# Winograd convolution on one core: the last stores of the seventh pair cut by rows and by channels

## The chip, the cores and the metric

The kernel runs on one core of one Trainium2 chip. The metric is the device time of one execution in microseconds (us), taken as a median over several executions. One further execution was recorded by the hardware profiler; every duration of an instruction, a transfer or a packet comes from it.

## The reference

A batch of 16 images of 64 channels, 64 by 64 pixels, is convolved with 128 filters of 64 channels, 3 by 3, with a border of one zero pixel. All is float32 in memory.

```python
batch, c_in, h, w, c_out = 16, 64, 64, 64, 128
x_pad = np.pad(x, ((0, 0), (0, 0), (1, 1), (1, 1)), mode='constant')
for b in range(batch):
    for co in range(c_out):
        for ci in range(c_in):
            for kh in range(3):
                for kw in range(3):
                    output[b, co] += weight[co, ci, kh, kw] * x_pad[b, ci, kh:kh+h, kw:kw+w]
```

The input has 16.8 MB, the output 33.6 MB.

## The kernel before, in words

Images are worked on in eight pairs (`p` from 0 to 7). The 64 channels of the first image of a pair lie on partitions 0 to 63, those of the second on 64 to 127 (`b2` is the image in the pair). Down the rows, a small Winograd scheme makes two output rows out of sums and differences of input rows: three matmul groups for each block of 16 output rows give `U` (from `ss`, sums of neighbouring rows), `A` and `Bt` (from `xs`, the rows in float16). ScalarE copies `U` into `ut` (L169), VectorE adds it to `A` for the even rows (L178) and to `Bt` for the odd rows (L181). The result lies in `ots[b2]`, one buffer for each image: 128 output channels on 128 partitions, with 64 rows of 64 float32 (16,384 bytes) on each. A pair has four blocks (`blk` 0 to 3, 16 rows each).

Loads: the first two pairs come in float32 by SyncE's queue (SP); the others are loaded by GpSimd's queue (POOL), which turns them into float16 on the way.

Stores: function `store` (L110) sends rows `lo` to `hi` of all 128 channels of one image. The first image of a pair goes out on SP, right after the block that makes its last row. The second image goes out on ScalarE's queue (ACT): it is put in the list `held` and issued in the next block, behind the copies of `U`. `cuts_of` (L108) says for each pair after which block which rows are sent: the first six pairs send each image whole (2 MB) after block 3. The seventh pair (`p = 6`) sends both images in halves (1 MB after block 1, 1 MB after block 3). The last pair (`p = 7`) sends its first image in three pieces (32, 16 and 16 rows after blocks 1, 2 and 3) and its second in halves.

The order of the instructions on each engine follows the order of the program; `keep` fixes it where it is called. The transfers on SP and ACT take turns over eight completion semaphores, so a transfer waits for the one that was issued eight such transfers before it. The eight output buffers are shared with the two float32 inputs, so pair `p` writes into the buffers of pair `p - 4`; the buffers of the last four pairs are not used again.

Of the kernel before, what the change touches and what calls it, by code (L numbers as in the profile page):

```python
# [13 lines left out]
def kernel(  # L14
# [6 lines left out]
    nc = tc.nc  # L21
    B, CI, H, W = x.shape
    CO = weight.shape[0]
    assert H == 64 and W == 64 and CI == 64 and CO == 128 and B % 2 == 0
    NP = B // 2
    RB = 8

    keep = tc.keep_in_program_order
    x_rows = x.rearrange("b c h w -> (b c) h w")
    out_rows = out.rearrange("b co h w -> b co h w")  # L30
# [24 lines left out]
    def load(p):  # L55
        xs[p] = xpool.tile([128, H, W], F16, tag="xs", name="xs")
        keep(nc.gpsimd.dma_start(xs[p], x_rows[128 * p : 128 * p + 128, :, :]))  # L57
# [8 lines left out]
    def sums(eng, p, src, lo, n):  # L66
        if p not in ss:
            ss[p] = spool.tile([128, H // 2, W], F16, tag="ss", name="ss")
        v = src.rearrange("p (j i) c -> p j i c", i=2)
        keep(  # L70
            eng.tensor_add(  # L71
                ss[p][:, lo : lo + n, :], v[:, lo : lo + n, 0, :], v[:, lo : lo + n, 1, :]
            )
        )
# [29 lines left out]

    whole = {3: (0, 64)}
    halves = {1: (0, 32), 3: (32, 64)}
    tail = {1: (0, 32), 2: (32, 48), 3: (48, 64)}
    cuts_of = [(whole, whole)] * (NP - 2) + [(halves, halves), (tail, halves)]  # L108

    def store(eng, p, b2, ot, lo, hi):  # L110
        return eng.dma_start(
            out_rows[2 * p + b2, :, lo:hi, :],
            ot.rearrange("p j i c -> p (j i) c")[:, lo:hi, :],
        )

    for p in range(NP):
        if p > 0 and p + 4 < NP:
            load(p + 4)
        if p + 1 < NP:
            for lo in (0, 16):  # L120
                sums(nc.gpsimd, p + 1, x1 if p == 0 else xs[p + 1], lo, 16)
        ots = [
            opool.tile([128, H // 2, 2, W], F32, tag="ot", name="ot") for _ in range(2)
        ]
        for blk in range(4):
            j0 = blk * RB

            def group(wi_rows):

                tiles = [  # L130
                    psum.tile([128, RB, W], F32, tag="acc", name="acc") for _ in range(2)
                ]
                n = 3 * len(wi_rows)
                i = 0
                for wi, off in wi_rows:
                    for kw in (1, 0, 2):
                        c_lo, c_hi = max(0, 1 - kw), min(W, W + 1 - kw)
                        for b2 in range(2):
                            p0 = 64 * b2
                            lo, hi = j0, j0 + RB  # L140
                            if off is None:
                                rhs = ss[p][p0 : p0 + 64, lo:hi, c_lo + kw - 1 : c_hi + kw - 1]
                            else:
                                while 2 * lo + off < 0:
                                    lo += 1
                                while 2 * (hi - 1) + off > H - 1:
                                    hi -= 1
                                first = 2 * lo + off
                                last = 2 * (hi - 1) + off
                                rhs = xs[p][  # L150
                                    p0 : p0 + 64,
                                    first : last + 1 : 2,
                                    c_lo + kw - 1 : c_hi + kw - 1,
                                ]
                            nc.tensor.matmul(  # L155
                                tiles[b2][:, lo - j0 : hi - j0, c_lo:c_hi],
                                Wt[p0 : p0 + 64, wi, kw, :],
                                rhs,
                                start=i == 0,
                                stop=i == n - 1,  # L160
                            )
                        i += 1
                return tiles

            U = group([(G1, None)])
            us = []
            for b2 in range(2):
                ut = upool.tile([128, RB, W], F32, tag="ut", name="ut")
                keep(nc.scalar.copy(ut, U[b2]))  # L169
                us.append(ut)  # L170
            while held:
                keep(store(nc.scalar, *held.pop(0)))
            if p == 0 and blk >= 2:
                for lo in (32 * blk - 64, 32 * blk - 48):
                    keep(nc.scalar.copy(xs[1][:, lo : lo + 16, :], x1[:, lo : lo + 16, :]))  # L175
            A = group([(G21, 1), (G0, -1)])
            for b2 in range(2):
                nc.vector.tensor_add(ots[b2][:, j0 : j0 + RB, 0, :], A[b2], us[b2])  # L178
            Bt = group([(G01, 0), (G2, 2)])
            for b2 in range(2):  # L180
                nc.vector.tensor_add(ots[b2][:, j0 : j0 + RB, 1, :], Bt[b2], us[b2])  # L181
            if blk in cuts_of[p][0]:
                store(nc.sync, p, 0, ots[0], *cuts_of[p][0][blk])
            if blk in cuts_of[p][1]:
                held.append((p, 1, ots[1], *cuts_of[p][1][blk]))
    while held:
        keep(store(nc.scalar, *held.pop(0)))
# [30 lines left out]
```

## Time and profile before

| what | value |
|---|---|
| median of 3 runs | 127.26 us (127.18 to 127.57) |
| profiled execution: its own time | 128.39 us |
| profiled execution: span, first to last instruction | 126.6 us |
| TensorE matmuls | 106.0 us busy, 84% of the span |
| VectorE | 83.6 us, 66% |
| ScalarE | 44.5 us, 35% |
| GpSimd | 34.6 us, 27% |
| last instruction of VectorE | starts at 115.77, takes 0.68 us |
| last store issued on SP / on ACT | 115.88 / 116.48 us |
| bytes moved, 16 DMA engines | 44.48 MB, mean 351 GB/s |

The profile has five views that matter here. The table in 40 slices shows how busy each engine and the mean of the 16 DMA engines are, 3.2 us to a slice. The list of DMA queues counts packets: q1 is SP's queue, q10 ACT's, q0 GpSimd's; a packet is one run of bytes that one DMA engine moves, and a transfer ends with one packet of 4 bytes on each DMA engine that took part. The chain of waits follows the work that ended last back in time. The table by stretch gives the DMA share (1.00 is all 16 DMA engines busy, so 0.0625 is one of them) for any stretch of time; a packet is counted in the stretch in which it begins, so values a little over 1 occur. The list of transfers gives the median time from issue to landing.

### The profile page before, as it was taken

How to read it: one execution, taken by the hardware profiler on the slowest of the kernel's cores; microseconds unless marked ns; L12 is line 12 of the kernel's file. 1: busy time of each engine (PE TensorE's matmuls, PEld its weight loads, DVE VectorE, ACT ScalarE, POOL GpSimd, SP SyncE). 2: the span in 40 equal slices, each digit the busy share in tenths (PEclk: the TensorE clock that was granted, in tenths of full speed). 3: DMA queues.
4: the chain of work that ended last, by engine and by line, in shares of the span. 5: the costliest groups of instructions: out<-in, count | busy, mean ns of one | idle time of the engine just before them, and what ended most of it. 6: DMA issues, size and time to landing. Idle time of an engine off the chain costs nothing.

```text
span 126.6 us, 2412 instructions
## 1 busy us (share of the span) xinstructions
PE 106.0 (84%) x978; PEld 54.3 (43%) x978; DVE 83.6 (66%) x134; ACT 44.5 (35%) x76; POOL 34.6 (27%) x27
## 2 busy tenths in 40 slices
PE   0407999999999999999999999999999999993000
PEld 0303454554555555554555545455554555541000
DVE  0009297787778777877787778777877787777000
ACT  4108937953333333333333333333333333330000
POOL 2700008677007700699770039000000000000000
PEclk9999999999999999999999999999999999999955
DMA  5999999999999999999999999999999999999970
GB/s 148 370 352 331 342 290 210 215 238 318 383 334 331 295 331 357 365 365 344 349 349 362 383 427 419 419 424 450 419 424 419 432 422 414 430 427 418 418 302 22
DMA packets 4330, 44.48 MB, mean 351 GB/s; under 512 B 480, under 2 KB 480, under 8 KB 864
## 3 DMA queue, kind: packets, MB, share of 16 engines
q1 hardware_dynamic: 2016, 21.27, 40.6%
q10 hardware_dynamic: 1440, 16.78, 31.7%
q0 software_dynamic: 864, 6.29, 24.1%
q8 instruction: 7, 0.11, 0.3%
q14 instruction: 3, 0.02, 0.0%
HBM read 17.07 MB, written 33.55 MB: 400 GB/s over the span
## 4 chain that ended last, share of the span: by engine, by line
PE 82%; DMA 7%; DVE 2%; issue 1%; DVEq 0%; SPq 0%
PE acc L155 82%; DMA x<-in_x_dram 7%; DVE ot L178 1%; DVE ss L71 1%; DVE ot L181 0%; DVEq L213 0%; SPq L42 0%; DVEq L178 0%
## 5 line engine op out<-in xcount | busy, mean ns | idle before, releaser
L155 PE MATMUL acc<-xs,Wt 64*128 64x504 f16 (+3 forms) x768 | 88.9, 378 | 0.0
L155 PEld LDWEIGHTS <-Wt 64*128 64x128 f16 x960 | 53.2, 95 | 55.9 <-issue 6.8
L178 DVE TENSOR_TENSOR ot<-acc,ut 128x512 f32<-128x512 f32 x64 | 41.2, 686 | 23.2 <-PE acc L155 18.5
L169 ACT COPY ut<-acc 128x512 f32<-128x512 f32 x64 | 34.4, 589 | 60.8 <-issue 38.5
L181 DVE TENSOR_TENSOR ot<-acc,ut 128x512 f32<-128x512 f32 x64 | 41.1, 685 | 0.0
L155 PE MATMUL acc<-ss,Wt 64*128 64x504 f16 (+1 forms) x192 | 27.0, 384 | 4.6 <-DVE ss L71 4.6
L71 POOL TENSOR_TENSOR ss<-xs 128x1024 f16<-128x1024 f16 x12 | 25.2, 2122 | 10.1 <-DMA xs<-in_x_dram 9.1
L71 DVE TENSOR_TENSOR ss<-x 128x512 f16<-128x512 f32 x4 | 2.6, 686 | 9.6 <-DMA x<-in_x_dram 9.6
L71 POOL TENSOR_TENSOR ss<-x 128x1024 f16<-128x1024 f32 x2 | 4.7, 2356 | 13.4 <-DMA x<-in_x_dram 13.4
L57 POOL DMA_DIRECT2D xs<-in_x_dram x6 | 3.5, 578 | 17.9 <-PE acc L155 16.0
L96 ACT CAST xs<-x 128x1024 f16<-128x1024 f32 (+2 forms) x4 | 4.0, 1053 | 4.0 <-DMA x<-in_x_dram 4.0
L89 PE MATMUL wp<-ident,w 128*64 128x128 f16 x18 | 1.3, 328 | 4.5 <-POOL w L51 4.5
L175 ACT CAST xs<-x 128x1024 f16<-128x1024 f32 x4 | 4.0, 1057 | 0.0
L89 PEld LDWEIGHTS <-w 128*64 128x64 f16 x18 | 1.1, 210 | 4.5 <-POOL w L51 4.5
L91 ACT CAST Wt<-wp 128x384 f16<-128x384 f32 x1 | 0.5, 478 | 3.1 <-PE wp L89 3.1
L91 ACT ACT_TABLE_LOAD x1 | 1.3, 1283 | 0.7 <-PEq L202 0.7
L51 POOL CAST w<-w_raw 128x576 f16<-128x576 f32 x1 | 0.7, 662 | 2.4 <-DMA w_raw<-in_weight_dram 2.4
L98 ACT CAST Wt<-wp 128x384 f16<-128x384 f32 x1 | 0.5, 478 | 0.5 <-DVE Wt L94 0.5
L93 DVE TENSOR_TENSOR Wt<-wp,Wt 128x384 f16<-128x384 f32 x1 | 0.6, 551 | 0.0
L94 DVE TENSOR_TENSOR Wt<-wp,Wt 128x384 f16<-128x384 f32 x1 | 0.5, 548 | 0.0
L99 ACT CAST Wt<-wp 128x384 f16<-128x384 f32 x1 | 0.5, 485 | 0.0
masks.py:199 POOL TENSOR_SCALAR_AFFINE_SELECT ident<-ident 128x128 f16<-128x128 f16 x1 | 0.3, 292 | 0.1
(5 smaller groups left out, 0.6 us busy)
## 6 DMA issues: line engine op xcount, KB each, us to landing
out_dram<-ot SPq DMA_DIRECT2D x6, 2048.0 KB, 19.7
out_dram<-ot ACTq DMA_DIRECT2D x6, 2048.0 KB, 19.3
xs<-in_x_dram POOLq DMA_DIRECT2D x6, 1024.0 KB, 20.5
x<-in_x_dram SPq DMA_DIRECT2D x2, 2048.0 KB, 13.1
out_dram<-ot ACTq DMA_DIRECT2D x4, 1024.0 KB, 11.7
out_dram<-ot SPq DMA_DIRECT2D x3, 1024.0 KB, 12.8
out_dram<-ot SPq DMA_DIRECT2D x2, 512.0 KB, 10.6
w_raw<-in_weight_dram SPq DMA_DIRECT2D x1, 288.0 KB, 3.0
```

What stands on the lines that cost most here:

```text
L51: keep(nc.gpsimd.tensor_copy(w16, w_raw))
L57: keep(nc.gpsimd.dma_start(xs[p], x_rows[128 * p : 128 * p + 128, :, :]))
L71: eng.tensor_add(ss[p][:, lo : lo + n, :], v[:, lo : lo + n, 0, :], v[:, lo : lo + n, 1, :])
L89: nc.tensor.matmul(wp[q : q + 64, k * CO : k * CO + CO], w16[:, t::9], ident)
L91: keep(nc.scalar.copy(wrow(G1), wps[1]))
L93: keep(nc.vector.tensor_sub(wrow(G21), wps[2], wrow(G1)))
L96: keep(nc.scalar.copy(xs[0][:, lo:hi, :], x0[:, lo:hi, :]))
L155: nc.tensor.matmul(tiles[b2][:, lo - j0 : hi - j0, c_lo:c_hi], Wt[p0 : p0 + 64, wi, kw, :], rhs, start=i == 0, stop=i == n - 1,)
L169: keep(nc.scalar.copy(ut, U[b2]))
L175: keep(nc.scalar.copy(xs[1][:, lo : lo + 16, :], x1[:, lo : lo + 16, :]))
L178: nc.vector.tensor_add(ots[b2][:, j0 : j0 + RB, 0, :], A[b2], us[b2])
L181: nc.vector.tensor_add(ots[b2][:, j0 : j0 + RB, 1, :], Bt[b2], us[b2])
```

## The change

Three things in the stores of the last two pairs change; the arithmetic and the loads stay as they are.

- Seventh pair, first image: rows 0 to 31 after block 1 as before. After block 3, rows 32 to 57 of all 128 channels in one transfer, then rows 58 to 63 in two: channels 0 to 123, and channels 124 to 127. All are on SP, in this order.
- Seventh pair, second image: one transfer of 64 rows (2 MB) after block 3 in place of two halves, on ACT.
- Last pair, first image: halves (after blocks 1 and 3) in place of 32, 16 and 16 rows. Its second image stays in halves.

On SP the order is now: six whole images, then transfers of 32, 26, 6 (124 channels), 6 (4 channels), 32 and 32 rows. On ACT: seven whole images, then two halves. The sequences of TensorE, VectorE and GpSimd are the same, and so is the number of transfers on SP and ACT together.

```diff
     whole = {3: (0, 64)}
     halves = {1: (0, 32), 3: (32, 64)}
-    tail = {1: (0, 32), 2: (32, 48), 3: (48, 64)}
-    cuts_of = [(whole, whole)] * (NP - 2) + [(halves, halves), (tail, halves)]
+    dealt = {1: (0, 32), 3: (32, 58)}
+    cuts_of = [(whole, whole)] * (NP - 2) + [(dealt, whole), (halves, halves)]

-    def store(eng, p, b2, ot, lo, hi):
+    def store(eng, p, b2, ot, lo, hi, c0=0, c1=CO):
         return eng.dma_start(
-            out_rows[2 * p + b2, :, lo:hi, :],
-            ot.rearrange("p j i c -> p (j i) c")[:, lo:hi, :],
+            out_rows[2 * p + b2, c0:c1, lo:hi, :],
+            ot.rearrange("p j i c -> p (j i) c")[c0:c1, lo:hi, :],
         )
...
             if blk in cuts_of[p][0]:
-                store(nc.sync, p, 0, ots[0], *cuts_of[p][0][blk])
+                keep(store(nc.sync, p, 0, ots[0], *cuts_of[p][0][blk]))
+                if p == NP - 2 and blk == 3:
+                    for c0, c1 in ((0, 124), (124, CO)):
+                        keep(store(nc.sync, p, 0, ots[0], 58, H, c0, c1))
```

## The prediction

> **What bounds the kernel now.** I read the slices first, then the chain of waits, the waits of SP, and the table by stretch over the end. The page:
>
> ```profile
> PE   0407999999999999999999999999999999993000
> DVE  0009297787778777877787778777877787777000
> DMA  5999999999999999999999999999999999999970
> DMA packets 4330, 44.48 MB, mean 351 GB/s; under 512 B 480, under 2 KB 480, under 8 KB 864
> q1 hardware_dynamic: 2016, 21.27, 40.6%
> q10 hardware_dynamic: 1440, 16.78, 31.7%
> q0 software_dynamic: 864, 6.29, 24.1%
> PE 82%; DMA 7%; DVE 2%; issue 1%; DVEq 0%; SPq 0%
> ```
>
> The chain is 82% TensorE, which would make matmuls the bound. But TensorE and VectorE are idle in the last three slices while the DMA row goes on, and SP's own waits say that its last line waits for stores:
>
> ```profile
> SPq L213 <- DMA out_dram<-ot: 9.1, 4, 4.3
> ```
>
> The table by stretch (columns: stretch, length, busy time of the five engines, clock, DMA share, GB/s) shows the rest:
>
> ```profile
> 92.00:104.00 12.00, 12.00 (x116) 6.15 (x114) 9.46 (x16) 4.22 (x8) 0.00 (x0) 1.00 1.00 425
> 104.00:116.00 12.00, 11.09 (x104) 5.44 (x100) 9.57 (x16) 3.29 (x7) 0.00 (x0) 1.00 1.01 424
> 119.00:121.50 2.50, 0.00 (x0) 0.00 (x0) 0.00 (x0) 0.00 (x0) 0.00 (x0) 0.80 1.02 426
> 121.50:122.20 0.70, 0.00 (x0) 0.00 (x0) 0.00 (x0) 0.00 (x0) 0.00 (x0) 0.50 0.85 357
> 122.20:122.90 0.70, 0.00 (x0) 0.00 (x0) 0.00 (x0) 0.00 (x0) 0.00 (x0) 0.50 0.49 205
> 123.10:123.80 0.70, 0.00 (x0) 0.00 (x0) 0.00 (x0) 0.00 (x0) 0.00 (x0) 0.50 0.20 82
> 123.90:124.10 0.20, 0.00 (x0) 0.00 (x0) 0.00 (x0) 0.00 (x0) 0.00 (x0) 0.50 0.10 41
> 124.20:125.10 0.90, 0.00 (x0) 0.00 (x0) 0.00 (x0) 0.00 (x0) 0.00 (x0) 0.50 0.07 27
> 125.30:126.60 1.30, 0.00 (x0) 0.00 (x0) 0.00 (x0) 0.00 (x0) 0.00 (x0) 0.50 0.00 0
> ```
>
> Up to 121.5 all 16 DMA engines work without a pause, so the end is set by what is left for them, not by when a store is issued. They do not end together. Sixteen times the share is the number still at work: 7.8 on average in 122.2 to 122.9, 3.2 from 123.1, one alone (0.07) from 124.2 to 125.2. Adding share times length from 121.5 on gives a mean end of about 122.7; the last engine is 2.5 us behind it. Its last store was issued at 115.88 and landed 9.8 us later, at 125.7; the span ends 0.9 later. The profiled execution took 128.39 us, 1.8 more than its span and 1.13 more than the median of 127.26; I carry the difference of the sum over to the median.
>
> How a transfer is dealt out can be counted: q1 has 2016 packets for 14 transfers, q10 1440 for 10, q0 864 for 6. All are 144 a transfer: 128 rows and 16 completion packets (480 under 512 B is 30 by 16). Each engine takes eight rows of every transfer, and has as many bytes as any other.
>
> **Prices of a packet.** A row of a transfer is one packet. From the counts of a stretch, share by 16 by length over packets:
>
> ```profile
> DMA packets 49, 0.11 MB, mean 376 GB/s; under 512 B 0, under 2 KB 0, under 8 KB 49
> q1 hardware_dynamic: 49, 0.11, 97.0%
> ...
> q1 hardware_dynamic: 93, 1.29, 50.6%
> ...
> q10 hardware_dynamic: 65, 0.52, 60.9%
> ...
> q1 hardware_dynamic: 6, 0.02, 6.6%
> ```
>
> Weights, 2.55 to 2.85: 0.97 x 16 x 0.3 / 49 = 95 ns for 2304 bytes. From 78 to 84: 48.6 us for 93 packets, about 14 of them completions: 0.61 us for 16,384. From 119 to 121: 19.5 us for 64: 305 ns for 8192. From 124.2 to 125.1: 0.95 / 6 = 158 ns for 4096. It is nearly a straight line with a few ns for each packet, so 6656 bytes (26 rows) cost 158 + (2560/4096) x 147 = 250 ns. The new packet of 1536 bytes (six rows) is smaller than any but completions: at least 57 ns (by bytes from 0.61 us), at most 95 (the 2304 packet); on the line it is 95 - 768 x 63/1792 = 68. I take 65, as the line is well marked on both sides of 2304.
>
> **The change, part by part.** (a) Rows 32 to 57 in place of 32 to 63: on every engine 8 x (250 - 305) = -0.44 us. (b) The six rows left: 128 packets of 65 ns, 8.3 us of engine time in all. The 124-channel transfer can't give eight rows to each of 16 engines. All 30 transfers in the trace are dealt in equal shares; the largest number of engines up to 16 that 124 divides by is 4, so I take 31 rows on each of four engines, and one row on each of four for the last four channels. If they are the same four: 32 x 65 = +2.08 us there (1.8 to 3.0 by the bounds), nothing elsewhere. The trace has no transfer of other than 128 rows, so the other ways of dealing are rivals below.
>
> [...]
>
> (c) Whole in place of halves: 8 x (607 - 2 x 305) = -0.02 us. (d) 32 rows in place of 16 and 16: 8 x (305 - 2 x 158) = -0.09 at most; packets of 4096 begin some 3 ns before the one ahead has ended, so -0.04 to -0.09. (e) Two completions fewer on 12 engines: -0.02. Sum: -0.53 us on twelve engines, +1.55 (1.3 to 2.5) on four.
>
> (f) Issues. SP has one more, ACT one fewer, 0.33 us each; SP has waited 109.8 us in all for VectorE, and its two new issues stand 6 us ahead of the next. The new waits are for transfers eight places back: the 124-channel piece for the fourth pair's second image, the 4-channel piece for the fifth pair's first, issued at 103; the later of these was issued before 78 and landed 17.7 us later, before 96. They cost nothing.
>
> (g) Later issues. 1 MB of the seventh pair's second image comes 6.6 us later (103.7 instead of 97), and rows 32 to 47 of the last pair 2.9 us later. The engines lose nothing while they have other work. The tightest place is the end: the last two stores are now 16 packets of 305 ns on each engine, 4.9 us, from 115.88 and 116.48. The first store of the kernel was issued at 26.2 and its packets began from 27.3 to 28.0, so I allow up to 1.8: work begins by 117.7 and 118.3. An engine that runs dry by then still ends at 118.3 + 4.9 = 123.2 at the latest. That is late for the early engines and free for the last one, which has work until 125.2 - 0.5 - 4.9 = 119.8 without them. If that cover were gone, the end could be no earlier than 123.2, so it is not what limits.
>
> The end: if none of the four is one of the three late engines, the last engine ends at 125.2 - 0.53 = 124.7, and the four at no more than 123.1 + 1.55. Both meet there, so the four just fit. The profiled execution would be 127.86, the median 126.73.
>
> **The rivals.** First, the one on the other side: the last engine is one of the four. Then the end moves by the whole +1.55: 128.8 us (128.6 at the low price). It decides from the place where one of the four ended later than 125.2 - 1.55 = 123.7 before. By blind draw the chance would be 4 in 16. Against it: in the first store packets began one engine after another, one in 27.3 to 27.6, five by 27.9, nine more by 28.1; engines that are served first would stay ahead, and a transfer for a few engines may well go to the first ones. I give 0.14. [...]
>
> Second: the second or third late engine, ending at 123.8 to 124.2, is one of the four: 125.35 to 125.75, or +0.1 to +0.5: 127.4 to 127.8. Chance 0.12.
>
> Third, the change does not do what it seems: the 124 rows are dealt over all engines, eight or seven each. Then every engine has 8 x (250 + 65 - 305) = +0.08 and -0.09 from (c) to (e): no change, 127.25. For it speaks only that nothing in the trace excludes it. 0.08.
>
> Fourth: 124 rows on one engine, 124 x 65 = 8 us on an engine that ended near 122.7: +5, or 132; on two, 62 x 65 = 4 us, +0.8. 0.04.
>
> Fifth: without the profiler the last engine is less late. The profiled execution is 1.13 us over the median; if all of it is the late engine, it ends at 124.1, the twelve at 123.6, and four that ended at 122.7 now end at 124.2: 127.3, no gain. For it: the difference itself. Against: 1.13 can as well lie ahead of the stores, where they begin. 0.10.
>
> **How the numbers follow.** Forecast 0.52, rivals 0.14, 0.12, 0.08, 0.04, 0.10. A difference of 0.3% (0.38 us) is about what a measurement of this kernel can tell from none. The forecast's own range is 126.4 to 127.0, and 0.43 of its 0.52 lies below 126.88. Faster: 0.43, and 0.02 of the fifth. Within: 0.09, 0.06 of the second, the third, and 0.08 of the fifth: 0.31. Slower: the first, the fourth and 0.06 of the second: 0.24. The range leaves out the first and fourth (0.18) and holds the others: 126.4 to 127.9. Nothing of the sum goes below: the twelve engines lose no more than half a microsecond.
>
> **What would show it.** In the changed profile: packets under 512 B down from 480 to 456 (four completions for each of the two short pieces, not 16); the DMA share at the end falling to nothing near 124.7, with several engines ending together between 124 and 124.7 instead of one alone. If a group of four works on alone after 125, the first or second rival holds. An end at 125.2 with nothing changed points to the third. If the span shrinks but the median doesn't, it is the fifth. The last stores of SP and ACT should still be issued at 115.9 and 116.5; an earlier or later VectorE would make the whole sum wrong.

## The result and the profile after

The changed kernel takes 127.93 us (median of 20 runs), the kernel before 127.19 us (20 runs beside them). The ratio is 1.0048, with a 95% interval of 1.0027 to 1.0069: slower by 0.3 to 0.9 us. The forecast was 126.73, with a range up to 127.9: the time lies just above the range, and the forecast had the sign wrong.

What the change does to the transfers is as forecast. The page of the changed kernel:

```profile
DMA  5899999999999999999999999999999999999981
DMA packets 4178, 44.48 MB, mean 355 GB/s; under 512 B 456, under 2 KB 584, under 8 KB 840
q1 hardware_dynamic: 2008, 21.27, 41.1%
q10 hardware_dynamic: 1296, 16.78, 31.6%
```

There are 456 packets under 512 bytes, 24 fewer than before: the two short transfers have four completions each (packets of 4 bytes at 109.29, 112.97, 113.20 and 113.32 us for the 124 channels, at 110.57, 113.04, 113.27 and 113.39 for the 4), so each ran on four DMA engines. Between 512 bytes and 2 KB are 128 packets, the six rows. SP's queue q1 has 13 transfers of 144 packets and 136 packets for the two short ones, 2008.

The waits of SP say, as before, that the end is a wait for stores:

```profile
SPq L216 <- DMA out_dram<-ot: 8.3, 4, 4.0
```

The table by stretch of the changed kernel (last two columns: share of the 16 DMA engines, GB/s):

```profile
92.00:104.00 12.00, 12.00 (x116) 6.12 (x112) 9.24 (x16) 4.30 (x8) 0.00 (x0) 1.00 1.00 423
104.00:116.00 12.00, 10.50 (x98) 5.14 (x94) 9.65 (x16) 3.22 (x6) 0.00 (x0) 1.00 1.00 412
119.00:121.50 2.50, 0.00 (x0) 0.00 (x0) 0.00 (x0) 0.00 (x0) 0.00 (x0) 0.63 0.94 397
121.50:122.20 0.70, 0.00 (x0) 0.00 (x0) 0.00 (x0) 0.00 (x0) 0.00 (x0) 0.50 0.33 140
122.20:122.90 0.70, 0.00 (x0) 0.00 (x0) 0.00 (x0) 0.00 (x0) 0.00 (x0) 0.50 0.25 105
123.10:123.80 0.70, 0.00 (x0) 0.00 (x0) 0.00 (x0) 0.00 (x0) 0.00 (x0) 0.50 0.14 59
123.90:124.10 0.20, 0.00 (x0) 0.00 (x0) 0.00 (x0) 0.00 (x0) 0.00 (x0) 0.50 0.00 0
```

Two things differ from before. In 122.2 to 122.9 the share is 0.25, four engines, where it was 0.49, and no single engine is left at the end: most engines end by 122, and a few go on to 124.0. (A share of 0.25 there is not yet proof of the four; see the six rows over 16 engines below.) And in 104 to 116, when the short transfers are under way, all engines are busy (1.00) but move 412 GB/s where they moved 424.

The last stores were issued at 115.29 and 115.89, 0.6 us earlier than in the first trace, which the prediction named as a sign that its sum is off. It is no steady effect of the change: in the three traces of the kernel before, the last store on SP is issued anywhere from 115.75 to 116.37, and in a second trace of the change at 115.77.

The traced execution of the changed kernel has a span of 125.3 us and took 127.05, the fastest of its 20; that of the kernel before took 128.39. In all 98 runs of the kernel before that stand beside these experiments the median is 127.24, and 8 are at 128.39 or above. So the two first traces are from opposite ends of their kernels' spread, and their spans must not be subtracted from one another. What follows rests on the timed comparisons, and on rates and counts inside the traces. Ratios compare fast runs alone, while medians hold the slow ones too, those more than 1.5% above the fastest of the same kernel, to which the first trace of the kernel before belongs.

### The profile page after: what moved, and what is told of

Same layout as the page of the kernel before. It is cut to its first block, busy times and chain, and to the rows that moved or that the text cites. A ratio compares the mean times of both kernels' runs of the same rounds, so it can differ in the third digit from the quotient of the medians.

```text
span 125.3 us, 2410 instructions
## 1 busy us (share of the span) xinstructions
PE 105.8 (84%) x978; PEld 54.2 (43%) x978; DVE 83.5 (67%) x134; ACT 44.6 (36%) x76; POOL 34.6 (28%) x27
## 4 chain that ended last, share of the span: by engine, by line
PE 82%; DMA 6%; DVE 2%; issue 1%; DVEq 0%; SPq 0%
PE acc L155 82%; DMA x<-in_x_dram 6%; DVE ot L178 1%; DVE ss L71 1%; DVE ot L181 0%; DVEq L216 0%; SPq L42 0%; DVEq L178 0%
```

## The experiments

Theory: in most executions no DMA engine is as late as the one in the first trace, so the four engines with 32 more packets become the last. Rival: the new cuts let the engines run dry, since 1 MB is issued 6.6 us later and 32 rows of the last pair 2.9 us later.

**The kernel before, traced twice more.** No edit.

> The kernel before, unchanged, for a second trace. Theory (the four): in most executions no DMA engine is as late as the one in the first trace, so here the last one ends about 1 us behind the mean of 122.7, near 123.5 to 124, and no engine works alone for a whole microsecond; time 127.2. Rival (the late stores): the single late engine at about 125 is there again, in every execution.

> The kernel before, unchanged, for one more trace of its end. Theory (single engines are late by an amount that changes from execution to execution): the last engine is 1 to 2 us behind the mean, at 123.5 to 124.5, and time 126.4 to 127.8. Rival (one engine is always 2.5 us late): an engine alone at work until about 125.

The first took 127.13 us (median of 10), ratio to its own kind 0.9968 (0.9939 to 0.9996): an interval that misses 1 by a hair for one and the same kernel, so differences of 0.3% are to be read with care here. The second, one execution, took 127.88. The ends of these two, first e1, then e5:

```profile
122.20:122.90 0.70, 0.00 (x0) 0.00 (x0) 0.00 (x0) 0.00 (x0) 0.00 (x0) 0.50 0.32 135
123.10:123.80 0.70, 0.00 (x0) 0.00 (x0) 0.00 (x0) 0.00 (x0) 0.00 (x0) 0.50 0.11 47
123.90:124.10 0.20, 0.00 (x0) 0.00 (x0) 0.00 (x0) 0.00 (x0) 0.00 (x0) 0.50 0.06 21
124.20:125.10 0.90, 0.00 (x0) 0.00 (x0) 0.00 (x0) 0.00 (x0) 0.00 (x0) 0.50 0.00 0
```

```profile
122.20:122.90 0.70, 0.00 (x0) 0.00 (x0) 0.00 (x0) 0.00 (x0) 0.00 (x0) 0.50 0.51 217
123.10:123.80 0.70, 0.00 (x0) 0.00 (x0) 0.00 (x0) 0.00 (x0) 0.00 (x0) 0.50 0.07 29
123.90:124.10 0.20, 0.00 (x0) 0.00 (x0) 0.00 (x0) 0.00 (x0) 0.00 (x0) 0.50 0.10 41
124.20:125.10 0.90, 0.00 (x0) 0.00 (x0) 0.00 (x0) 0.00 (x0) 0.00 (x0) 0.50 0.03 14
```

The last engine ends at 124.1 in the one and near 124.7 in the other, against 125.2 in the first trace; I had expected 124.0 and 124.5 at the latest. In e1 no single engine is left alone. In e5 one is, from 123.1 to 124.7, nearly as the rival had it. By the shares the last engine is 1.8, 2.3 and (in the first trace) 2.5 us behind the mean. So some engine is late in all three, by an amount that changes, and the first trace had the latest end.

**The dealing taken out, the cuts kept.** Against the change, the six rows go in one transfer of 128 channels; run twice.

```diff
-                    for c0, c1 in ((0, 124), (124, CO)):
+                    for c0, c1 in ((0, CO),):
```

> The change with its last six rows in one transfer of 128 channels, so dealt over all 16 DMA engines. Theory (the four engines carry 1.55 us more and become the last): the loss goes, 127.0 to 127.3, within 0.2 of the kernel before. Rival (the later issue of the seventh pair's second image and of the last 32 rows lets engines run dry): still 127.8 to 128.0.

> The kernel with the six rows in one transfer over all 16 engines, a second time beside the others. Theory: each engine has 0.05 us less work than before, so no difference that can be measured, 127.0 to 127.3. Rival (the first result of 0.997 was a gain): 126.8 to 126.95 again.

126.93 us, ratio to the kernel before 0.9971 (0.9935 to 1.0006), and 127.14, ratio 0.9992 (0.9956 to 1.0027). The loss is gone. In the two traces 104 to 116 is back at 424 and 422 GB/s, with the same number of packets of 1536 bytes. The first of them, with its end:

```profile
104.00:116.00 12.00, 10.49 (x98) 6.45 (x93) 9.47 (x16) 3.22 (x6) 0.00 (x0) 1.00 1.01 424
122.20:122.90 0.70, 0.00 (x0) 0.00 (x0) 0.00 (x0) 0.00 (x0) 0.00 (x0) 0.50 0.25 105
123.10:123.80 0.70, 0.00 (x0) 0.00 (x0) 0.00 (x0) 0.00 (x0) 0.00 (x0) 0.50 0.00 0
```

The share in 122.2 to 122.9 is 0.25 here too, where no engine has more to do than another. So that value in the trace of the change does not show the four; what differs is that here nothing is left after 123.3.

**The dealing alone, the cuts of before.** Against the change:

```diff
+    tail = {1: (0, 32), 2: (32, 48), 3: (48, 64)}
...
-    cuts_of = [(whole, whole)] * (NP - 2) + [(dealt, whole), (halves, halves)]
+    cuts_of = [(whole, whole)] * (NP - 2) + [(dealt, halves), (tail, halves)]
```

> Only the six rows are dealt by 124 and 4 channels; the seventh pair's second image goes in halves and the last pair's first image in 32, 16 and 16 rows, as before. Theory (the four): the whole loss is here, 127.8 to 128.1. Rival (the late stores): as the kernel before, 127.0 to 127.3.

127.70 us, ratio 1.0042 (1.0003 to 1.0081): the loss is there without the new cuts, though the interval clears 1 by a hair only. Its trace ends not with a group of four but with one engine alone, until 125.1. The records have no numbers of engines, but on one engine a packet begins 3 to 4 ns before the one ahead of it ends, so an engine's packets can mostly be followed one by one. Followed like this, the engine that works alone is one that carried the short transfers, until 114.5.

**The new cuts alone.** Against the kernel before:

```diff
-    cuts_of = [(whole, whole)] * (NP - 2) + [(halves, halves), (tail, halves)]
+    cuts_of = [(whole, whole)] * (NP - 2) + [(halves, whole), (halves, halves)]
```

> The new cuts without the dealing: the seventh pair's first image in halves, its second whole, the last pair in halves. Theory (what counts is each engine's work, and fewer packets are less work): 0.05 to 0.15 us less work on every engine, 127.0 to 127.2, same as before within the measurement. Rival (the later issues cost): 127.5 or more.

127.32 us, ratio 1.0002 (0.9973 to 1.0031). The later issues cost nothing that can be measured, and the fewer packets bring nothing that can be measured. These four results, with that of the change, settle that the dealing by channels is the cause of the loss. They don't yet say by which way it costs time.

**Another dose.** Against the change, twelve rows, then three, in place of six.

```diff
-    dealt = {1: (0, 32), 3: (32, 58)}
+    dealt = {1: (0, 32), 3: (32, 52)}
...
-                        keep(store(nc.sync, p, 0, ots[0], 58, H, c0, c1))
+                        keep(store(nc.sync, p, 0, ots[0], 52, H, c0, c1))
```

(For three rows, 61 stands in both places.)

> Twelve rows in place of six go by 124 and 4 channels. Theory (the four): they carry about 2.9 us more than a store of halves would give them, so the end moves by another 1.3 to 1.5 us beyond the change: 129.2 to 129.5. Rival (the late stores): no further loss, 127.8 to 128.0.

> Three rows in place of six go by 124 and 4 channels. Theory (the four): twelve engines have 0.25 to 0.35 us less than before, the four 0.6 to 1.0 more, by the line of packet prices; between the kernel before and the change: 127.2 to 127.6. Rival (the short transfers themselves cost, whatever their size): as with six rows, 127.8 to 128.0.

Twelve rows: 129.81 us, ratio 1.0153 (1.0104 to 1.0202). By the ratios this is 1.05% beyond the change, 1.3 us, as expected; by the medians, over six runs here, it is 1.9, more than expected. Its end shows the group most plainly:

```profile
121.50:122.20 0.70, 0.00 (x0) 0.00 (x0) 0.00 (x0) 0.00 (x0) 0.00 (x0) 0.50 0.28 117
122.20:122.90 0.70, 0.00 (x0) 0.00 (x0) 0.00 (x0) 0.00 (x0) 0.00 (x0) 0.50 0.22 94
123.10:123.80 0.70, 0.00 (x0) 0.00 (x0) 0.00 (x0) 0.00 (x0) 0.00 (x0) 0.50 0.22 94
124.20:125.10 0.90, 0.00 (x0) 0.00 (x0) 0.00 (x0) 0.00 (x0) 0.00 (x0) 0.50 0.13 55
125.30:126.60 1.30, 0.00 (x0) 0.00 (x0) 0.00 (x0) 0.00 (x0) 0.00 (x0) 0.50 0.02 6
```

0.22 by 16 is 3.5, four engines with small gaps in the count, and they work alone from 122.2 to 123.8; two go on until after 125.3. From 117 on the packets can be followed on all 16 engines without a break: twelve end at 121.0 to 122.0 and four at 123.9, 124.2, 125.6 and 125.8. Three of the four still send short packets after 116.5, and on the last two both short transfers end, one behind the other, before the last two stores begin. So here the four are shown. Three rows: 126.86 us, ratio 0.9978 (0.9944 to 1.0013), better than expected and the same as before. So the dose decides: 3 rows nothing that can be measured, 6 rows +0.5%, 12 rows +1.5%. A bend between three and six is what to expect if the four first have to catch up with the late engine, but the intervals are too wide to show one.

**The changed kernel, traced once more.** No edit.

> The changed kernel, unchanged, for one more trace. Theory (the four): the four engines that completed the short transfers are again the last or nearly so, ending at 123 to 125, the others by 123. Rival (chance: the four were late in that one execution): the last engines are others.

One execution, 127.56 us. Engines are at work until 124.5 and the share is 0.36 in 122.2 to 122.9 and 0.17 in 123.1 to 123.8: no clear group of four here. Followed packet by packet, the last engine but one, which ends at 124.3, carried the short transfers, and so did two that end at 122.5 and 123.3; for the very last, at 124.5, the records don't tell. So the four are not the last four as a group. The rate in 104 to 116 is 413 GB/s, as in the first trace.

**Another deal: 120 and 8 channels, half an image.** Against the kernel before, with `store` taking channels as in the change:

```diff
-    cuts_of = [(whole, whole)] * (NP - 2) + [(halves, halves), (tail, halves)]
+    dealt = {1: (0, 32)}
+    cuts_of = [(whole, whole)] * (NP - 2) + [(dealt, halves), (tail, halves)]
...
+            if p == NP - 2 and blk == 3:
+                for c0, c1 in ((0, 120), (120, CO)):
+                    keep(store(nc.sync, p, 0, ots[0], 32, H, c0, c1))
```

> The kernel before, but rows 32 to 63 of the seventh pair's first image go as 120 and 8 channels. If shares are equal on the largest number of engines up to 16 that divides, 120 channels run on 15 engines and 8 on 8: one engine is left out of 8 packets of 8192 bytes (2.4 us), eight engines get one more (0.3 us), so 15 and 8 completions. Theory (which engine is late changes): one engine ends 2 us or more ahead of all others, and time is 127.2 to 127.6, no better than before. [...]

128.63 us, ratio 1.0085 (1.0046 to 1.0123): slower than the theory had it. There are 487 completions, 480 less 16 plus 23, as many as 15 and 8 engines give. Its table:

```profile
104.00:116.00 12.00, 10.45 (x97) 5.31 (x93) 9.42 (x16) 3.22 (x6) 0.00 (x0) 1.00 1.00 383
119.00:121.50 2.50, 0.00 (x0) 0.00 (x0) 0.00 (x0) 0.00 (x0) 0.00 (x0) 0.51 1.02 424
121.50:122.20 0.70, 0.00 (x0) 0.00 (x0) 0.00 (x0) 0.00 (x0) 0.00 (x0) 0.50 0.73 304
```

The theory's sign in the trace did not come either: no engine ended 2 us ahead of all others, though by that count one was spared 2.4 us. Followed packet by packet, the first ends at 121.1 and the next at 121.6. The spared one may have been a late one, or longer packets may have hidden it; this is not shown. But eight engines got only 0.3 us more, 0.24% of the time, and the kernel lost 0.85%. The rest is in the first line: 383 GB/s with every engine busy, where (424 - 383)/424 of 12 us is 1.2 us of every engine.

**Equal shares from other channels.** The loss of rate was tested by itself. Against the run with 120 and 8 channels:

```diff
-                for c0, c1 in ((0, 120), (120, CO)):
+                for c0, c1 in ((0, 64), (64, CO)):
```

> The kernel before, but rows 32 to 63 of the seventh pair's first image go as 64 and 64 channels: four packets for each of the 16 engines from each, so every engine has the same work as before, but from other channels than in a transfer of 128. Theory (which channels an engine reads beside the others stretches the packets, as seen from 104 to 116 where the bytes fell from 424 to 412 GB/s in the change and 383 with 120 and 8): fewer than 415 GB/s from 104 to 116 and 127.5 to 128.5. Rival (unequal shares alone stretch them): 420 GB/s or more, 127.1 to 127.4.

128.40 us, ratio 1.0082 (1.0047 to 1.0118). All 16 engines take part in both transfers (496 completions, 16 more than before), so at equal shares the bytes on each engine are those of the kernel before:

```profile
92.00:104.00 12.00, 12.00 (x116) 6.13 (x114) 9.24 (x16) 4.30 (x8) 0.00 (x0) 1.00 0.99 422
104.00:116.00 12.00, 10.63 (x100) 5.15 (x96) 9.78 (x16) 3.22 (x6) 0.00 (x0) 1.00 1.01 371
```

From 422 to 371 GB/s at full share: the packets themselves last longer. In the packet records of 104 to 116, 76 of the 277 packets of 8192 bytes on q1 were recorded at over 15 ns more than the usual 309, the longest at 1.38 us, 21 us more in all. So this loss came with all 16 engines in both pieces: here a store that was split by channels cost time beside other stores, with the same bytes on each engine if shares are equal.

## Why the prediction was wrong, point by point

**What bounds the kernel** held. In three traces of the kernel before no engine ends before 121.2, the end is a wait for stores, and moving issues by 3 to 7 us changed nothing: parts (c), (d) and (g) together are the cuts alone, 1.0002.

**The dealing** held, as far as completions were counted: 4 and 4 for 124 and 4 channels, 23 in all for 120 and 8 (15 and 8 at equal shares on the largest number that divides), 16 and 16 for 64. The prediction took this from 30 transfers of 128 channels, an estimate then. That the two short transfers share their engines, on which its +1.55 rests, was an assumption that no trace had shown; the trace of the change shows it for all four: on three engines the completion of the 124 channels, one row and the completion of the 4 follow one another within 0.1 us (from 112.97, 113.20 and 113.32), on the fourth the row comes at 109.90 and its completion at 110.57, each behind one packet of ACT's store. In the trace with twelve rows it is shown for two engines. The third and fourth rival are out. Which of the sixteen the four are no record shows.

**The end** is the step that failed: "if none of the four is one of the three late engines, the last engine ends at 125.2 - 0.53", with the four just under it. It took the end of one engine in one execution for a property of the kernel, and carried the difference over to the median. That execution took 1.13 us more than the median, and two further traces had the last engine at 124.1 and 124.7. With less to gain from the twelve, the four decide. This is the fifth rival's mechanism, to which I gave 0.10, although the 1.13 us stood in the text as its evidence; its time of 127.3 was too low as well, for the reason that follows.

**The price of the six rows** is the mis-sized term. I took 65 ns for a packet of 1536 bytes, and that is what one takes when the rows are dealt over all 16 engines (65.0 ns on average). Dealt over four they took 82.4 ns in the trace of the change, 77.5 in its second trace and 72.8 with the dealing alone, since some were stretched (in the first of these to as much as 313 ns). So the four carried 32 x 82 = 2.6 us, or +2.1 us after parts (a), (c) and (d), not +1.55 (+1.8 at 72.8). It lay inside my bounds of 1.3 to 2.5, but "both meet there, so the four just fit" left no room for it.

The size fits, by an estimate. Take the ends of the 16 engines, followed packet by packet, in each of the three traces of the kernel before; add 2.1 us to four of them, never the last one, take 0.53 from the others, and average over all choices of the four: the end moves by +0.3 us in the first trace and by +1.1 and +0.4 in the other two. With 1.55 in place of 2.1 it is -0.1, +0.6 and -0.1. Measured was +0.3 to +0.9. So both errors count, the end taken from one execution and the price. This is worked out from three traces, not shown.

One more way stands beside it. In 104 to 116 the other packets were stretched too: over the usual time of their size they took 0.2 to 0.4 us of each engine in the three traces with six rows dealt over four engines, against 0.1 before. No run takes this apart from the work of the four at six rows; with twelve rows it is 0.1, and there the four carry the loss.

**The other rivals.** The first (the last engine is one of the four) would have given 128.8 in every execution; the median is 127.93, so it is not the rule, though a single execution may have been so. The second (127.4 to 127.8) comes near the time, but it rests on the late engines of the first trace, and which engines are late and which are the four no record shows: it stays open. **The argument that engines served first stay ahead**, and that a transfer for a few engines goes to the first ones, can't be tested on these traces: no record has the number of an engine.

## What to carry to other kernels

Where DMA engines are full to the end, balance between them can count (here twelve rows on four engines cost 1.5%), but a late engine must be seen in several traces, and its execution compared with the median, before bytes are moved around it. In a kernel like this one, keep stores at all 128 channels: in the splits by channels tried here the rate beside other stores fell (371 to 417 GB/s in 104 to 116, against 422 to 425), and in most of them fewer engines shared a transfer (4 for 124 channels, all 16 still for 64), while a split by rows of all channels cost nothing that can be measured (0.9971, 0.9992 and 1.0002). No version tried is clearly faster than the kernel before: three rows dealt (0.9944 to 1.0013) and six rows over 16 engines (0.9935 to 1.0006, then 0.9956 to 1.0027) can't be told from it.

## What the runs showed of the hardware that was not expected

Beside another queue's stores, transfers of all 128 channels keep 16 engines at 419 to 425 GB/s over 12 us; the same bytes as 64 and 64 channels fall to 371 in the 12 us around them, as 120 and 8 to 383, and a far smaller part (six rows) as 124 and 4 to 407 to 413 in three traces, at a full share of busy engines each time. The loss in the 64 and 64 case, (422 - 371)/422 of 12 us or 1.45 us of every engine, is of the size of the measured 0.6 to 1.5 us. What stretched the packets stays open: no run here shows which partitions an engine read.
